# A diffusion block's feed-forward: gate folded into the second weights, sums begun as the residual, context products kept in two PSUM banks

## The chip, the cores and the metric

One core of a Trainium2 chip runs the whole kernel. The metric is the device time of one execution in microseconds (us). Five engines work side by side, each with its own queue that it works off in order: PE (matrix products), ACT, DVE and POOL (element by element), and SP, which here issues loads. POOL issues the stores and some loads.

## The reference, cut to what matters

One layer runs over 128 context tokens and 2,048 latent tokens, 17 tiles of 128. The change lies in the feed-forward part and the end:

```python
h = rmsnorm(x, norm2_g) * (1 + scale2) + shift2
x = x + gate2 * (jnp.square(jax.nn.relu(h @ w_ff1)) @ w_ff2)
...
y_prompt = rmsnorm(y_p, final_g)
y_sample = rmsnorm(y_s, final_g)
```

`w_ff1` is 1024 x 4096 and `w_ff2` 4096 x 1024. `gate2` has 1,024 columns, one row for the context token tile and one for all latent tiles. Ahead of it lie the mixing part and its output projection (`out_proj`).

## The kernel before, in words

Every product of two f32 operands is made of three matmuls (`mm3`, L179): both operands are split into a high and a low part (`split`, `operand`), and high x high, high x low and low x high are added in one PSUM bank. Over this the latent tiles use a seven-product scheme for 2 x 2 blocks: sums of operand blocks are formed first, seven products (numbered p = 0 to 6) are made, and their results are added up.

**FF1** (L1330 to L1391) makes `relu(h @ w_ff1)**2`. Its outer loop g runs over two halves of the latent tokens, its inner loop i over 16 slices of 256 columns of `w_ff1`; one pair (g, i) is called a step here. A step (`ff1_units`, L1249) has 7 products of 4 units, 84 matmuls of 512 columns in all, and in the first half (g = 0) also 24 matmuls of 256 columns for the context tile. Products 0, 2, 4 and 6 add up in one bank (`za`), 3 and 5 in another (`zc`): product 4 can't start before the sum after product 2 has been copied out. These sums go to three buffers, `fx` (two of it), `fy` and `fz` (one each): f00 and f10 in `fx`, f01 and f11 in `fz`; POOL forms the operand sums of FF2 in `fy` and `fz` (`comb`, L1265), and POOL's queue stores all three to DRAM (`f_d`, L1287, L1292, L1293). While a step runs, the weights of the next are loaded, added and split (`left_operand`), and twice in the second half `w2_prep` (L1347) forms sums of `w_ff2`'s blocks for FF2 on POOL and stores them in `w2_d`.

**FF2** (L1396 to L1599) runs over 8 chunks c of 512 rows of `w_ff2`, and in each over four blocks b of four token tiles with 28 units, 84 matmuls, each, and a fifth, the context tile (`ff2_context`, 24 matmuls). `operand` loads each operand (SP), casts it on ACT (L1413) and subtracts on DVE or POOL by turns (L1414). `put` (L1447) adds each finished bank to the tile's sum `ya` on DVE, or in the first and last chunk copies it on ACT (L1459). `whole` (L1465) runs in the last two chunks: it multiplies the sum by the gate row (DVE), adds the residual `x1_d` or the older sum (POOL), and in the last chunk squares (ACT) for the final norm. `norm` (L1485) scales and stores.

The order of the work is written out by hand in `weave` (L154): a list of PE's units, and beside it items with the unit number ahead of which each is put in the program. The framework may still move an instruction that isn't pinned with `keep_in_program_order`; matmuls and the `ld_in_order` loads are pinned. A tile of a ring waits until all uses of the tile that had its place before are over.

Of the kernel before, what the change touches and what calls it, by code (L numbers as in the profile page):

```python
# [12 lines left out]
ALU = mybir.AluOpType  # L13
# [30 lines left out]
def tile_hybrid(  # L44
# [39 lines left out]
    w2_d = [dram.tile([P, 2, 2, D], F32, name=f"w2_d{c}") for c in range(DFF // 512)]  # L84
# [1096 lines left out]
    for t in range(NT - 2, -1, -1):  # L1181
# [67 lines left out]
    def ff1_units(g, i, w, tb):  # L1249
# [8 lines left out]
        f00, f10, f01, f11 = fx[:, 0], fx[:, 1], fz[:, 0], fz[:, 2]  # L1258
# [9 lines left out]
        def after(p):  # L1268
# [66 lines left out]
    for i, kk in ORDER[4:6]:  # L1335
        right_operand(0, i, kk, TB[0])
# [10 lines left out]
    def w2_prep(i, unit):  # L1347


        box = []  # L1350

        def load():
            for f in range(2):
                box.append(unit())
                ld.dma_start(out=box[f], in_=w_ff2[0, (2 * i + f) * P:(2 * i + f + 1) * P, :])

        def step():
            (x, y), (z, w) = ((b[:, 0:512], b[:, 512:]) for b in box)
            G.tensor_tensor(out=w, in0=w, in1=y, op=ALU.subtract)
            G.tensor_tensor(out=y, in0=y, in1=x, op=ALU.subtract)  # L1360
            G.tensor_tensor(out=x, in0=w, in1=x, op=ALU.add)
            G.tensor_tensor(out=z, in0=z, in1=x, op=ALU.subtract)
            for f in range(2):
                st.dma_start(out=w2_d[i // 2][:, i % 2, f], in_=box[f])

        return load, step

    for g in range(2):
        for i in range(NP):
# [26 lines left out]
    gp = ctx.enter_context(tc.tile_pool(name="gp", bufs=1, reuse_waits="tile"))  # L1396
    CP = 2
    NC_ = NP // CP
    ya, yl, norms, ctr = {}, {}, [], [0]

    def ounit(dt=F32R):
        return gp.tile([P, D], dt, tag="o", name="o", bufs=24)

    def sunit(dt=F32R):
# [225 lines left out]
```

## Time and profile before

| | us |
|---|---|
| median of 3 runs (2595.0 to 2604.34) | 2604.31 |
| the profiled execution | 2596.67 |
| its span, first to last instruction | 2594.9 |
| PE busy | 2319.6 (89%) |
| DVE busy | 1804.1 (70%) |
| POOL busy | 1141.9 (44%) |
| ACT busy | 979.7 (38%) |

The rows below are from this one execution. FF1 runs from about 985 to 1826 us of the span, its second half from about 1402, and FF2 from there to the end. L131 is the line of every matmul, so PE's rows are told apart by their tiles: `z` and `g` are PSUM banks, `T`, `u`, `v`, `o` and `s` operand tiles. A busy PE isn't PE at its peak, since the ends of matmuls are modelled; the number of matmuls in a stretch, in brackets, is the better measure.

### The profile page before, as it was taken

The numbers are of one execution on the slowest core, as the hardware profiler recorded it, in microseconds if no ns is written. First come the engines' busy times: TensorE is split into PE (matmuls) and PEld (weight loads), VectorE is DVE, ScalarE is ACT, GpSimd is POOL, SyncE is SP. The second block draws the span as 40 slices with busy tenths as digits, with TensorE's granted clock in tenths as the row PEclk, the third lists the DMA queues.
The fourth block names the chain that finished last, engine by engine and source line by source line (L and its number), as shares of the span: only waits on it lengthen the run. The fifth ranks groups of instructions, "written<-read, shape, count | busy, mean of one in ns | idle before, by whom it ended". The sixth has DMA issues, their size and how long they took to land.

```text
span 2594.9 us, 32716 instructions
## 1 busy us (share of the span) xinstructions
PE 2319.6 (89%) x12018; PEld 1876.3 (72%) x12018; DVE 1804.1 (70%) x2632; ACT 979.7 (38%) x1824; POOL 1141.9 (44%) x1023
## 2 busy tenths in 40 slices
PE   7999999999979897999996788888799999999766
PEld 5788887777757675777775566667588778787655
DVE  5987755878878847667766665655347776778887
ACT  4666663333435455322323222222342222222243
POOL 1332225444324454334435633434544554347764
PEclk9999999999989997999998898889899999999888
DMA  8666444333355555343335423333655555455633
GB/s 279 218 216 204 172 153 143 120 122 126 135 189 181 178 196 176 116 140 132 110 132 196 165 100 124 103 121 110 219 177 176 198 207 178 164 182 195 226 124 116
DMA packets 212655, 422.75 MB, mean 163 GB/s; under 512 B 16165, under 2 KB 116815, under 8 KB 208912
## 3 DMA queue, kind: packets, MB, share of 16 engines
q1 hardware_dynamic: 166704, 246.27, 29.0%
q0 software_dynamic: 45792, 174.40, 19.1%
q8 instruction: 95, 1.56, 0.2%
q14 instruction: 64, 0.52, 0.1%
HBM read 267.76 MB, written 152.85 MB: 162 GB/s over the span
## 4 chain that ended last, share of the span: by engine, by line
PE 39%; POOL 16%; DVE 12%; DMA 11%; issue 8%; ACT 4%; POOLq 0%; SPq 0%; DVEq 0%; ACTq 0%
PE z L131 29%; PE g L131 9%; DMA f_d<-fz 6%; POOL fy L1266 4%; POOL fz L1266 4%; DVE cacc L67 3%; DMA o<-f_d 1%; PE g L134 1%; DMA raw<-in_w_ff_dram 1%; POOL o L1414 1%; DVE v L177 1%; DVE fz L67 1%; DMA T<-tb_d 1%; POOL f_d L1287 1%; POOL T L1482 1%
## 5 line engine op out<-in xcount | busy, mean ns | idle before, releaser
L131 PE MATMUL z<-w,hb 128*128 128x512 f32 (+1 forms) x2486 | 564.5, 373 | 13.8 <-ACT hb L776 7.4
L131 PEld LDWEIGHTS z<-w,hb 128*128 128x128 f32 x2486 | 420.0, 191 | 95.5 <-ACT hb L776 7.6
L131 PE MATMUL z<-u,v 128*128 128x512 f32 x1152 | 305.7, 428 | 87.7 <-ACT fz L1275 83.5
L131 PEld LDWEIGHTS z<-u,v 128*128 128x128 f32 x1152 | 238.9, 210 | 154.1 <-ACT fz L1275 96.0
L131 PE MATMUL z<-o 128*128 128x512 f32 x1152 | 299.9, 411 | 54.6 <-ACT o L1459 25.4
L131 PE MATMUL z<-T,v 128*128 128x512 f32 x1152 | 290.2, 405 | 35.9 <-DVE T L1171 13.0
L131 PEld LDWEIGHTS z<-o 128*128 128x128 f32 x1152 | 227.5, 199 | 111.2 <-ACT o L1459 27.5
L131 PEld LDWEIGHTS z<-T,v 128*128 128x128 f32 x1152 | 221.6, 194 | 90.2 <-DVE T L1171 13.8
L131 PE MATMUL g<-o 128*128 128x512 f32 x1152 | 278.9, 391 | 0.8 <-DVE T L1461 0.7
L1413 ACT CAST o<-o 128x1024 fp32r<-128x1024 f32 x128 | 134.3, 1051 | 384.6 <-DMA o<-f_d 276.4
L131 PEld LDWEIGHTS g<-o 128*128 128x128 f32 x1152 | 217.5, 189 | 48.5 <-DVE T L1461 1.3
L1266 POOL TENSOR_TENSOR fy<-fz 128x512 f32<-128x512 f32 x32 | 60.2, 1880 | 424.8 <-DVE fz L67 424.8
L67 DVE SCALAR_TENSOR_TENSOR cacc<-xp,wd,cacc 128x512 f32<-128x512 f32 (+2 forms) x360 | 237.4, 713 | 0.0
L1414 POOL TENSOR_TENSOR o<-o 128x1024 fp32r<-128x1024 f32 x49 | 120.2, 2452 | 204.7 <-ACT o L1413 204.4
L1461 DVE TENSOR_TENSOR T<-T,z 128x512 f32<-128x512 f32 x212 | 141.9, 681 | 72.9 <-PE z L131 72.7
L131 PE MATMUL z<-w,T 128*128 128x512 f32 x720 | 183.5, 409 | 7.4 <-POOL T L777 3.8
L1461 DVE TENSOR_TENSOR T<-T,g 128x512 f32<-128x512 f32 x167 | 113.5, 683 | 80.2 <-PE g L131 68.4
L1414 DVE TENSOR_TENSOR o<-o 128x1024 fp32r<-128x1024 f32 x79 | 139.5, 1766 | 36.8 <-ACT o L1413 36.8
L131 PEld LDWEIGHTS z<-w,T 128*128 128x128 f32 x720 | 136.1, 194 | 38.6 <-POOL T L777 4.7
L177 DVE TENSOR_TENSOR v<-cacc,v 128x1024 fp32r<-128x1024 f32 x64 | 98.6, 1542 | 73.1 <-PE z L131 73.1
L177 DVE TENSOR_TENSOR v<-raw,v 128x1024 fp32r<-128x1024 f32 x64 | 117.2, 1832 | 42.6 <-PE z L131 40.0
L131 PE MATMUL z<-o,s 128*128 128x512 f32 x528 | 132.1, 402 | 13.5 <-DVE T L1461 6.8
(317 smaller groups left out, 3795.6 us busy)
## 6 DMA issues: line engine op xcount, KB each, us to landing
raw<-in_w_ff_dram SPq DMA_DIRECT2D x116, 512.0 KB
o<-f_d SPq DMA_DIRECT2D x96, 512.0 KB
f_d<-fz POOLq DMA_DIRECT2D x32, 768.0 KB, 5.9
raw<-in_w_mod_dram SPq DMA_DIRECT2D x32, 512.0 KB
f_d<-fy POOLq DMA_DIRECT2D x32, 512.0 KB, 3.5
f_d<-fx POOLq DMA_DIRECT2D x32, 512.0 KB, 3.6
o<-w_d SPq DMA_DIRECT2D x32, 512.0 KB
hb<-hT_d POOLq DMA_DIRECT2D x15, 1024.0 KB, 5.7
```

What stands on the lines that cost most here:

```text
L67: return V.scalar_tensor_tensor(out=out, in0=in0, scalar=scalar, in1=in1, op0=op0, op1=op1)
L131: tc.keep_in_program_order(T.matmul(out, lhsT, rhs, start=start, stop=stop, skip_group_check=read))
L134: tc.keep_in_program_order(T.transpose(out, in_, ident if idn is None else idn))
L177: order(V.tensor_tensor(out=lo, in0=src, in1=hi.bitcast(F32), op=ALU.subtract))
L1266: G.tensor_tensor(out=out, in0=a, in1=b, op=op)
L1287: st.dma_start(out=dst[:, 2:4], in_=fy)
L1413: S.copy(out=hi, in_=lv)
L1414: (G if ctr[0] % 2 else V).tensor_tensor(out=lo, in0=lv, in1=hi.bitcast(F32), op=ALU.subtract)
L1461: V.tensor_tensor(out=o_, in0=o_, in1=bank, op=ALU.add)
L1482: eng.tensor_tensor(out=y[:, fs], in0=y[:, fs], in1=tmp, op=ALU.add)
```

## The change: what it does, and the diff

In FF1, f01 is kept in `fy` and the copy of product 3 too; only the sum after product 4 goes to `fz`. The three POOL sums stand in another order. The right operand i = 2 of the first half is loaded while `out_proj` works on tile 0, and the first operands of FF2 in the last step of FF1. `w2_prep` multiplies the rows of `w_ff2` by the latent gate row on POOL and stores all seven combinations of each, so `w2_operand` reads them all from `w2_d`. In FF2 every sum `ya` begins as the residual, loaded from `x1_d` in the first chunk, and each bank is added on DVE; `put` and `whole` are gone. The context tile's fifth block is gone: in each block b two units (six matmuls) on plain rows of `w_ff2` add to two PSUM banks that are held through all of FF2, and its gate and residual are applied at the end. Cut to what matters:

```diff
-    w2_d = [dram.tile([P, 2, 2, D], F32, name=f"w2_d{c}") for c in range(DFF // 512)]
+    w2_d = [dram.tile([P, 2, 7, 512], F32, name=f"w2_d{c}") for c in range(DFF // 512)]
...
-        if t in (3, 1):
+        if t in (3, 1, 0):
 
-            items += [(10 + 4 * kk, lambda kk=kk, i=(3 - t) // 2: right_operand(0, i, kk, TB[0])) for kk in range(2)]
+            items += [((10 if t else 5) + 4 * kk, lambda kk=kk, i={3: 0, 1: 1, 0: 2}[t]: right_operand(0, i, kk, TB[0]))
+                      for kk in range(2)]
...
-        f00, f10, f01, f11 = fx[:, 0], fx[:, 1], fz[:, 0], fz[:, 2]
+        f00, f10, f01, f11 = fx[:, 0], fx[:, 1], fy[:, 1], fz[:, 2]
...
             elif p == 3:
-                S.copy(out=f11, in_=zc)
+                S.copy(out=fy[:, 0], in_=zc)
             elif p == 4:
-                V.tensor_tensor(out=f11, in0=f11, in1=za, op=ALU.add)
+                V.tensor_tensor(out=f11, in0=fy[:, 0], in1=za, op=ALU.add)
                 square(f11)
             elif p == 5:
                 V.tensor_tensor(out=f01, in0=f01, in1=zc, op=ALU.add)
                 square(f01)
+                comb(fz[:, 0], f00, f01, ALU.subtract)
                 comb(fy[:, 1], f01, f11, ALU.add)
                 comb(fy[:, 0], fy[:, 1], f00, ALU.subtract)
-                comb(fz[:, 0], f00, f01, ALU.subtract)
                 st.dma_start(out=dst[:, 2:4], in_=fy)
...
-    for i, kk in ORDER[4:6]:
-        right_operand(0, i, kk, TB[0])
...
-    def w2_prep(i, unit):
+    def w2_prep(i, unit, g2):
...
-                ld.dma_start(out=box[f], in_=w_ff2[0, (2 * i + f) * P:(2 * i + f + 1) * P, :])
+                ld_in_order(out=box[f], in_=w_ff2[0, (2 * i + f) * P:(2 * i + f + 1) * P, :])
+
+        def gate():
+            for x in box:
+                G.tensor_tensor(out=x, in0=x, in1=g2, op=ALU.mult)
+            st.dma_start(out=d_[:, 0], in_=box[0][:, 0:512])
+            for f, p in ((0, 1), (1, 5)):
+                st.dma_start(out=d_[:, p], in_=box[1][:, f * 512:f * 512 + 512])
...
+            for p, o in ((2, x), (4, y), (3, w), (6, z)):
+                st.dma_start(out=d_[:, p], in_=o)
...
+            if (g, i) == (1, NP - 1):
+
+                items += [(x, lambda n=n: f_operand(0, 0, n, F, tunit)) for x, n in ((5, 0), (9, 1), (15, 2))]
+                items.append((11, lambda: w2_operand(0, 0, w2, tunit)))
+            if g == 1 and i == 3:
+                g2f = raw()
+                gate_row(g2f, 1, 1)
             if g == 1 and i in (4, 8):
-                items += zip((3, 12), w2_prep(i // 4 - 1, lambda: tunit(F32)))
+                items += zip((3, 10, 22), w2_prep(i // 4 - 1, lambda: tunit(F32), g2f))
...
-            put(c, t, hs, bank, first)
-            if p == 1:
-                whole(c, e, 0)
...
+            y = ya[t][:, (left, right)[h]]
+            V.tensor_tensor(out=y, in0=y, in1=bank, op=ALU.add)
+            if last and p in (1, 4, 5, 6):
+                square(t, h)
+            if last and norms and (p < 5 or b == 3):
                 norm(norms.pop(0))
...
+    def residual(b):
+
+        for t in sum([[e, e - 1] for e in tiles_of(b)], []):
+            ya[t] = tunit(F32)
+            ld_in_order(out=ya[t], in_=x1_d[t])
...
-    def ff2_context(c, F, w2):
...
+    yc = [zbank(), zbank()]
+
+    def context(c, b, Fc):
...
+        def load():
+            rw = raw()
+            k = 2 * CP * c + b
+            ld_in_order(out=rw, in_=w_ff2[0, k * P:(k + 1) * P, :])
+            box.extend([ounit(), ounit()])
+            split_two(*box, rw)
+
+        def unit(h):
+            hs = (left, right)[h]
+            mm3(yc[h], *Fc[b % 2, b // 2], box[0][:, hs], box[1][:, hs], c + b == 0, (c, b) == (NC_ - 1, 3), True)
...
+    w2_operand(0, 1, w2)
+    residual(0)
+    for p in range(2, 7):
         w2_operand(0, p, w2)
+    f_operand(0, 0, 3, F)
+    fc_operand(0, Fc)
...
-        for b in range(5):
+        for b in range(4):
             items, Fn = [], {}
-            units = ff2_units(c, b, F, w2) if b < 4 else ff2_context(c, F, w2)
+            units = ff2_units(c, b, F, w2)
+            cload, cunits = context(c, b, Fc)
+            units[16:16] = cunits
+            items.append((3, cload))
...
+            if b == 0 and c > 0:
+                items += wl(c, (0.5, 5), (5, 6), w2)
+            if c == 0 and b < 3:
+                items.append((8, lambda: residual(b + 1)))
+            if b in (0, 1) and more:
+                items += zip((6, 12, 26), w2_prep(CP * (c + 1) + b, raw, g2r))
```

`split_two` casts on ACT and subtracts on POOL or DVE by turns, as `operand` did. The gate row is held in one of the three `raw` tiles (`g2f`) in FF1 and in a `cacc` tile in FF2.

## Rows read from the trace of the kernel before

**Rows 1.** Busy time by stage (start:end, span; engines; granted clock, DMA share, GB/s).

```profile
1052.90:1360.00 307.10, 290.44 (x1401) 240.16 (x1400) 211.57 (x203) 89.34 (x128) 121.58 (x103) 0.99 0.39 128
1445.00:1826.00 381.00, 318.81 (x1256) 254.93 (x1255) 225.13 (x217) 86.69 (x114) 144.50 (x112) 0.90 0.34 120
1827.00:1872.00 45.00, 28.84 (x86) 20.91 (x87) 16.83 (x13) 15.64 (x21) 28.03 (x18) 0.77 0.65 220
1934.00:2352.70 418.70, 411.89 (x1806) 337.82 (x1805) 297.79 (x356) 114.60 (x122) 198.60 (x121) 1.00 0.56 187
2352.70:2595.00 242.30, 184.13 (x718) 145.66 (x716) 201.00 (x245) 77.07 (x141) 164.61 (x113) 0.87 0.48 163
```

**Rows 2.** Waits of PE: total us, times, longest.

```profile
PE z L131 <- ACT fz L1275: 83.5, 29, 6.2
PE z L131 <- ACT o L1459: 28.5, 6, 7.2
```

**Rows 3.** Timeline, two steps of FF1's second half (start, us, engine, what, idle before).

```profile
1615.08 0.59 ACT L1275 COPY fz<-z 128x512 f32<-128x512 f32 x1 [10.01 <-DMA f_d<-fz]
...
1615.72 9.91 PE L131 MATMUL z<-u,v 128*128 128x512 f32 x36 [3.98 <-ACT fz L1275]
...
1625.47 2.93 PE L131 MATMUL z<-T,v 128*128 128x512 f32 x12
...
1625.91 2.21 POOL L1266 TENSOR_TENSOR fy<-fz 128x512 f32<-128x512 f32 x1 [15.61 <-DVE fz L67]
...
1631.47 0.75 POOL L1287 DMA_DIRECT2D f_d<-fy  x1
...
1634.43 0.77 POOL L1293 DMA_DIRECT2D f_d<-fz  x1
1636.51 1.23 DVE L177 TENSOR_TENSOR v<-cacc,v 128x1024 fp32r<-128x1024 f32 x1 [2.20 <-PE z L131]
...
1640.42 0.59 ACT L1275 COPY fz<-z 128x512 f32<-128x512 f32 x1 [10.45 <-DMA f_d<-fz]
```

**Rows 4.** Timeline, PE in two steps of FF1's first half.

```profile
1184.55 8.45 PE L131 MATMUL z<-u,v 128*128 128x512 f32 x36 [1.12 <-ACT fz L1275]
...
1208.23 8.46 PE L131 MATMUL z<-u,v 128*128 128x512 f32 x36 [1.11 <-ACT fz L1275]
```

**Rows 5.** Timeline, PE in FF1's first step.

```profile
999.48 0.80 PE L131 MATMUL z<-T,v 128*128 128x512 f32 x1 [4.18 <-ACT T L1170]
```

**Rows 6.** Page, DMA issues: KB each, us to landing.

```profile
f_d<-fy POOLq DMA_DIRECT2D x32, 512.0 KB, 3.5
```

**Rows 7.** Timeline, end of FF1 and start of FF2.

```profile
1826.52 0.37 SPq L137 DMA_DIRECT2D o<-f_d  x1
...
1833.52 2.35 POOL L1414 TENSOR_TENSOR o<-o 128x1024 fp32r<-128x1024 f32 x1
1835.83 2.36 POOL L1414 TENSOR_TENSOR o<-raw,o 128x1024 fp32r<-128x1024 f32 x1
...
1835.93 4.63 PE L131 MATMUL z<-o 128*128 128x512 f32 x10 [4.16 <-POOL o L1414]
```

**Rows 8.** Groups of POOL instructions from 1840 to 2350 us (busy, mean ns).

```profile
L1414 POOL TENSOR_TENSOR o<-o 128x1024 fp32r<-128x1024 f32 x38 | 92.0, 2421 | 195.3 <-ACT o L1413 195.1
...
L1362 POOL TENSOR_TENSOR raw<-raw 128x512 f32<-128x512 f32 x12 | 23.3, 1943 | 0.9
...
L1364 POOL DMA_DIRECT2D w_d<-raw x24 | 13.4, 558 | 0.0
```

**Rows 9.** Groups of DVE instructions from 1840 to 2350 us.

```profile
L1461 DVE TENSOR_TENSOR T<-T,z 128x512 f32<-128x512 f32 x177 | 118.6, 682 | 59.9 <-PE z L131 59.7
```

**Rows 10.** Line 1414 from 1840 to 2350 us (ns min/median/max).

```profile
L1414 DVE TENSOR_TENSOR o<-o x62: 1211/1226/4055, 1842.8 to 2349.7; 128x1024 fp32r<-128x1024 f32 x62
```

**Rows 11.** Groups of ACT instructions from 2470 to 2595 us.

```profile
L64 ACT ACTIVATE o<-T 128x512 f32<-128x512 f32 x34 | 21.5, 632 | 50.1 <-POOL T L1482 47.9 <-DVE T L1482 2.3
```

**Rows 12.** Groups of DVE instructions from 2470 to 2595 us.

```profile
L67 DVE SCALAR_TENSOR_TENSOR T<-T,ssq,cacc 128x512 f32<-128x512 f32 x34 | 31.0, 945 | 11.3 <-POOL ssq L166 11.3
```

**Rows 13.** Timeline, PE's last products.

```profile
2577.82 4.60 PE L131 MATMUL z<-o,s 128*128 128x512 f32 x12 [3.11 <-ACT o L1459]
```

More of the change, by code (lines that the diff above doesn't have):

```diff
@@ new lines, in w2_prep, with ounit, sunit, split_two @@
+        return load, gate, step
+    CP = 2
+    NC_ = NP // CP
+    gp, ya, yl, norms, ctr = [], {}, {}, [], [0]
+    w2, F, Fc = {}, {}, {}
+    def ounit(dt=F32R):
+        return gp[0].tile([P, D], dt, tag="o", name="o", bufs=24)
+    def sunit(dt=F32R):
+        return gp[0].tile([P, 512], dt, tag="s", name="s", bufs=6)
+    def split_two(hi, lo, src):
+        ctr[0] += 1
+        S.copy(out=hi, in_=src)
+        (G if ctr[0] % 2 else V).tensor_tensor(out=lo, in0=src, in1=hi.bitcast(F32), op=ALU.subtract)
@@ L1363, in step, with fc_operand @@
+    def fc_operand(c, out):
+        x = operand(fc_d[c].rearrange("p q f n -> p (q f) n"), sunit)
+        for q in range(2):
             for f in range(2):
-                st.dma_start(out=w2_d[i // 2][:, i % 2, f], in_=box[f])
-        return load, step
+                out[f, q] = [y[:, (2 * q + f) * P:(2 * q + f + 1) * P] for y in x]
     for g in range(2):
@@ L1391, in tile_hybrid @@
     fps.close()
[L1396 to L1404, printed above, removed]
-        return gp.tile([P, 512], dt, tag="s", name="s", bufs=6)
-    def operand(src, unit, via=None):
-        hi, lo = unit(), unit()
-        lv = lo.bitcast(F32) if via is None else via()
-        ld_in_order(out=lv.rearrange("p (a n) -> p a n", a=src.shape[1]), in_=src)
-        ctr[0] += 1
-        S.copy(out=hi, in_=lv)
-        (G if ctr[0] % 2 else V).tensor_tensor(out=lo, in0=lv, in1=hi.bitcast(F32), op=ALU.subtract)
-        return hi, lo
@@ L1427, in f_operand @@
[L1427 to L1440 removed]
+    gp.append(ctx.enter_context(tc.tile_pool(name="gp", bufs=1, reuse_waits="tile")))
@@ L1442, in tile_hybrid @@
     fgr = cacc()
     ld.dma_start(out=fgr, in_=final_g.unsqueeze(0).broadcast_to([P, D]))
-    g2rows = {1: cacc()}
-    gate_row(g2rows[1], 1, 1)
-    def put(c, t, hs, bank, first):
-        last = c == NC_ - 1
-        if last:
-            if t not in yl:
-                yl[t] = ounit(F32)
-            o_ = yl[t][:, hs]
-        else:
-            if t not in ya:
-                ya[t] = tunit(F32)
-            o_ = ya[t][:, hs]
-        if first and (last or c == 0):
-            S.copy(out=o_, in_=bank)
-        else:
-            V.tensor_tensor(out=o_, in0=o_, in1=bank, op=ALU.add)
@@ L1463, in tile_hybrid @@
[L1463 to L1483 removed]
+    g2r = cacc()
@@ new lines, in tile_hybrid, with tiles_of, square @@
+    gate_row(g2r, 1, 1)
+    left, right = slice(0, 512), slice(512, 1024)
+    def tiles_of(b):
+        return [NT - 1 - 8 * (b // 2) - 4 * (b % 2) - 2 * j for j in range(2)]
+    def residual(b):
+        for t in sum([[e, e - 1] for e in tiles_of(b)], []):
+            ya[t] = tunit(F32)
+            ld_in_order(out=ya[t], in_=x1_d[t])
+    def square(t, h):
+        if t not in yl:
+            yl[t] = const.tile([P, 2], F32, name="ssq4", bufs=8)
+        fs = (left, right)[h]
+        act(raw4[0][:, fs], ya[t][:, fs], AF.Square, accum_out=yl[t][:, h:h + 1])
@@ L1497, in ff2_units @@
     def ff2_units(c, b, F, w2):
-        units = []
         banks = {}
-        tt = [NT - 1 - 8 * (b // 2) - 4 * (b % 2) - 2 * j for j in range(2)]
+        tt = tiles_of(b)
+        last = c == NC_ - 1
         def after(p, j):
```

162 lines of the change are left out of this document (57 added, 105 removed).

## The prediction

> **What bounds the kernel now.** I read the busy time by stage first, then PE's waits, then the timeline inside the stages that lose time. By stage [rows 1] PE runs 1,806 matmuls in 411.89 busy us in FF2's chunks 1 to 5, so 0.228 us for one of 512 columns at granted clock 1.00, the 2.4 GHz level. A stage is judged against that price. Chunks 1 to 5 take 418.7 / 5 = 83.7 us each, against 360 x 0.228 = 82.1: PE bounds them. FF1's second half takes 381 / 15 = 25.4 us a step (1,256 matmuls recorded, 15 x 84 = 1,260) against 84 x 0.228 = 19.15. The first block of FF2 takes 45 us for 84 matmuls, and the last two chunks and the tail 242.3 us for 720, that is for 164.2. In these three the granted clock is 0.90, 0.77 and 0.87, so some of the time ran at 1.2 GHz.
>
> PE's waits [rows 2] name two causes: 83.5 us in 29 waits for the copy of line 1275 (f01 into `fz`), and 28.5 us in 6 for the copies of line 1459, which `put` makes in the last chunk. The timeline of FF1 [rows 3] shows the first. The copy sits on ACT until the store of the previous step's `fz` has landed: issued at 1634.43, copy at 1640.42. Product 4 needs the same bank, so PE stands. A step is then a loop: landing, products 4 to 6, POOL's sums, store, landing; 25.3 us from one copy to the next. In the first half the context tile's 24 matmuls lie inside the loop, and the wait is 1.1 us [rows 4] at clock 0.99.
>
> **FF1's second half.** After the change f01 is copied to `fy`, whose store comes earlier. Counted from product 0 at 1625.47 [rows 3], POOL starts at +0.4, issues the `fy` store at +6.0 and the `fz` store at +9.0. The new order of the three sums has the same three sums ahead of the first. The `fy` store takes 3.5 us to land [rows 6], so the place is free at +9.5 and the copy done at +10.1. Product 4 is due at 4 x 12 x 0.228 = +10.9, so this wait would be gone, with 0.8 us to spare. `fz` is needed only for the sum after product 4, at +13.7; its store lands at +15.0 (the copy at 1640.42 shows it), and product 6, which needs the bank, is due at +16.4: the sum of 0.7 us [rows 9] just fits. Next late is the low part of a weight: DVE writes it at 1636.51 to 1637.74, +11.0 to +12.3, after a wait of 2.2 us for PE. Product 4's third matmul would want it at +11.4, if this is the weight of product 4 and keeps its place: 0.9 us. With 0.4 us for DVE, which is blocked in front of `fz`'s sum from +13.7 to +15, a step is 19.15 + 1.3 = 20.5. The term is 15 x (25.4 - 20.5) = -74. Bounds: 19.2 a step (-93), or half of the difference kept, 22.3 (-47).
>
> The two `w2_prep` of this half grow. Each gets 2 POOL products of 1,024 columns; no row shows a POOL product with a gate row, so I bound it by the split of the same width, 2.42 us, and by twice the 512-column difference, 3.9 [rows 8], and take 2.4, since it is the same shape. Its stores go from 2 to 7 at 0.56. That is 4.8 + 2.8 = 7.6 us each on POOL, which works 144.50 / 15 = 9.6 us in a step [rows 1] and so has about 11 free. If a gate stands ahead of the sums, PE pays. The gate row also holds one of the three `raw` tiles, so a load of weights starts up to half a step later, ahead of ACT's casts. +8 for both (0 if POOL's gap covers it, +25 if each costs most of a step).
>
> **FF1's first half and start.** The first half has the same loop and loses its 1.1 us in 14 steps: -15 (0 to -16). At the start PE waits 4.2 us for a cast of the right operand that is now made earlier [rows 5]: -5 (0 to -10). The two loads and splits move behind the output projection's POOL work and delay nothing that I see; if POOL is late there, the gain is 0.
>
> **FF2's first block.** PE is through with FF1 at about 1826.5, when the next operand load is let go [rows 7], and then waits mostly for operands. Now product 0's operands are split before that, so PE goes on. Product 1's low part is on POOL, behind FF1's last sums and stores, which let POOL go at 1833.52: ready at 1835.9, 9.4 us after FF1. From there PE needs 72 x 0.228 = 16.4, and the rest of the operands come at the pace of casts of 1 us, so the block ends 26 to 27 us after FF1, not 45: -18 (-8 if the loads behind the four residuals on SP come late, -24 if nothing is missed).
>
> **Chunks 0 to 5.** Matmuls stay the same: 24 of the context in each chunk either way. POOL's work grows from 198.6 / 5 = 39.7 us a chunk [rows 1] by two context splits (4.8), four gate products (9.6) and 10 stores (5.6): about 60 of 82, so it doesn't bound by sum. DVE gets two more splits and loses three sums and some more, about even at 297.8 / 5 = 59.6. SP's loads gain the context's plain rows and lose nothing; DMA was at a share of 0.56. Three orders can cost. A context split given to POOL stands behind the second part of `w2_prep`, 4 differences and 4 stores, about 8 us, and is wanted after 16 of 30 units, 10.9 us. The next `raw` loads wait for those stores, and the FF2 operands behind them on SP. And the two context banks are held, so only two `z` banks are left for product 0: at each block's start it waits for the sum of product 6, 0.69 us [rows 9], with 6 matmuls, 1.37 us, as cover; a DVE split in front of it (1.23 us at the median [rows 10]) uncovers about half a us. Against this go 1.6 us of today's loss a chunk. I take +10 over six chunks (-8 to +35).
>
> **Chunks 6 and 7 and the tail.** `whole` goes: 64 gate products on DVE and 64 adds on POOL, and the copies on ACT that wait behind squares, which themselves waited 47.9 us for POOL's adds [rows 11]. Chunk 6 becomes like chunk 5, 83.7. Chunk 7 has no `w2_prep`, but DVE makes 14 sums of 0.69, about 4 us of splits and four norms a block. A norm is two products of 0.945 us and a wait of 11.3 / 17 [rows 12], 2.6 us, and all four are called in the first four units after a block: 10.4 us of DVE beside 5.5 us of PE. PE has cover of some 6 us before product 4 wants a bank, so about 2.5 us are lost in each of three blocks: 82 + 8 = 90. The tail was 2594.9 - 2582.4 = 12.5 us after the last product [rows 13] and becomes about 11: a sum, a square, two norms, a store. Together 185 against 242.3: -57 (-42 to -66).
>
> **The sum.** -5 - 15 - 74 + 8 - 18 + 10 - 57 = -151, from the profiled execution's 2596.67 to 2446. That execution is 7.6 us below the median of the runs shown, 2604.31, and close to the lowest, 2595.0; I give 2445 and leave the offset to the range. About 0.5%, 13 us, is what a measurement of this kernel can tell from no change.
>
> **A rule against it.** DVE's split of 1,024 columns takes 1.23 us at the median and 1.21 at the least, but 4.06 at the most [rows 10]: now and then it is held up by about a POOL split (2.42 us), mostly it isn't. The Trainium skill (SBUF — State Buffer, section Who interferes with whom) says that a DVE instruction with two SBUF inputs and a GpSimd one that reads SBUF exclude each other for the whole instruction. By that rule, POOL's 20 us more a chunk would meet a quarter of the 14 DVE splits and hold each up by half an instruction, 4 us of DVE a chunk; if all of it reached PE, six chunks would cost 24 us more and the sum would be 2470. The long instances agree with it; the median shows that it is rare here.
>
> **The rivals.** First, **a new wait in FF1's loop**: `fy`'s landing or the late weight takes over. For it: margins of 0.8 and 0.7 us, and DVE at 225 of 381 us and blocked in order. Against it: the `fy` store is issued 3 us before the `fz` store and lands 2.4 us faster. With half of the gain gone, 36 + 8 more: about 2490; chance 0.18. Second, **POOL's queue in FF2's chunks**: the context split and the loads behind `w2_prep` stop PE by about 8 us in each of seven chunks, 56 less the 10 counted: 2491; chance 0.18. Third, **all covers hold**: second half 19.2 a step, `w2_prep` free, chunks 82.1, first block at its best: 2446 - 19 - 8 - 20 - 6 = 2393; chance 0.14. Fourth, **slower than before by the held banks**: at each of 31 block borders both halves of product 0 wait behind a DVE split at its longest, 4.06 + 0.69 - 1.37 = 3.4 us each, 6.8 a border, 210 us and so 2656. It decides from 151 / 31 = 4.9 us a border. Against it: the median split is a third of that, and a split ready early is placed after the sums. Chance 0.03. That the wait of line 1275 goes on as it was, because the framework keeps ACT behind `fz` all the same, would leave 2446 + 89 = 2535; nothing in the code does this: 0.02.
>
> **How the numbers follow.** The forecast has 0.45, from 2415 to 2475 by its own terms. The range takes in half of the third case and the first two: 2390 to 2515; about 0.18 is left out, above and below. Faster by over 0.5% are all cases but the fourth and some mixture of the second with a poor start: 0.95; same 0.02, slower 0.03.
>
> **What would show it.** Right: the wait of PE for line 1275 below 10 us in all; 84 matmuls each 20 to 21 us in FF1's second half, clock 0.97 or more; first FF2 block below 30 us; no line 1459; POOL about 60 us in a chunk of 83 to 86; last two chunks and tail 180 to 195. Wrong: a step above 22 us with PE waiting for DVE's weights or the copy into `fy`; PE waiting for POOL's context split at unit 16 of block 1; PE waiting for DVE at block borders for over 2 us.

## The result, and the profile after

The changed kernel takes 2481.26 us in the median of four runs (2473.83 to 2484.8), the kernel before 2604.32 beside it: a ratio of 0.9532, interval 0.9501 to 0.9562. Direction and range held; the gain is 123 us instead of the 159 forecast. The profiled execution's span goes from 2594.9 to 2480.1 us, 114.8 less. The stages are cut at POOL's stores of `fz`, which end a step of FF1, and at PE's products in FF2:

| stretch | before | after | difference | predicted |
|---|---|---|---|---|
| to the first `fz` store | 1034.1 | 1038.2 | +4.1 | -5 |
| FF1, first half, 15 steps | 388.3 | 367.0 | -21.3 | -15 |
| the step between the halves | 32.6 | 26.5 | -6.1 | 0 |
| FF1, second half, 15 steps | 377.7 | 311.7 | -66.0 | -66 |
| FF2, first block | 45.0 | 42.3 | -2.7 | -18 |
| FF2, the rest of chunks 0 to 5 | 480.7 | 503.8 | +23.1 | +10 |
| FF2, chunks 6 and 7, tail | 242.3 | 196.9 | -45.4 | -57 |

(FF2's first row begins where FF1's last matmul ends; half a us lies between the landmarks.) FF1 gave 89 us, FF2 25 where 65 were forecast.

The busy time by stage of the changed kernel (columns as in [rows 1]): FF1's halves, the first block of FF2, chunks 1 to 5, and the rest.

```profile
1066.20:1405.20 339.00, 322.23 (x1558) 269.30 (x1556) 260.35 (x236) 112.60 (x154) 152.71 (x129) 0.97 0.45 148
1431.70:1743.40 311.70, 291.39 (x1239) 235.91 (x1237) 229.38 (x212) 93.76 (x120) 162.47 (x134) 0.97 0.51 174
1737.10:1779.40 42.30, 26.07 (x92) 19.96 (x91) 19.66 (x19) 14.81 (x16) 38.17 (x29) 0.80 0.98 357
1844.80:2288.90 444.10, 421.00 (x1811) 341.35 (x1810) 336.62 (x352) 134.84 (x140) 314.86 (x202) 0.99 0.65 217
2288.90:2480.10 191.20, 164.52 (x700) 132.34 (x698) 137.65 (x207) 64.72 (x112) 93.82 (x66) 0.95 0.54 186
```

In chunks 1 to 5 POOL now works 315 of 444 us, 63 a chunk (it was 39.7), as forecast; the chunk takes 88.8 us instead of 83.2 (from one cast of a `raw` operand in the chunk's first block to the same one of the next chunk, mean of five; the figure used for chunks from here on). In the first block DMA is at a share of 0.98.

The waits of PE:

```profile
PE z L131 <- DVE T L1498: 24.3, 20, 3.2
PE z L131 <- DVE o L1389: 21.2, 7, 8.3
PE z L131 <- ACT fy L1276: 15.0, 5, 6.6
...
PE g L131 <- POOL o L1389: 6.4, 1, 6.4
```

Both lines of [rows 2] are gone: 112 us of waits. In their place stand DVE's sums into the residual (L1498), the low parts of operands (L1389) and some of the copies into `fy`. The timeline of a quiet step of FF1's second half answers to [rows 3]:

```profile
1639.15 2.88 PE L131 MATMUL z<-T,v 128*128 128x512 f32 x12
...
1645.47 0.75 POOL L1288 DMA_DIRECT2D f_d<-fy  x1 [0.30 <-POOL fy L1267]
...
1649.53 0.59 ACT L1276 COPY fy<-z 128x512 f32<-128x512 f32 x1 [5.92 <-DMA f_d<-fy]
...
1650.17 8.45 PE L131 MATMUL z<-u,v 128*128 128x512 f32 x36
...
1658.46 2.88 PE L131 MATMUL z<-T,v 128*128 128x512 f32 x12
```

ACT still waits for a landing, now that of `fy`, 4.1 us after its issue; the copy ends at +10.97 from product 0, and product 4 starts at +11.02 without a wait. The step takes 19.31 us, the price of its 84 matmuls.

FF2's first block waits for operands (timeline, first block and, last two rows, what was late):

```profile
1746.65 5.06 PE L131 MATMUL g<-o,T 128*128 128x512 f32 x11 [6.44 <-POOL o L1389]
...
1767.67 2.50 PE L131 MATMUL z<-o,s 128*128 128x512 f32 x5 [8.29 <-DVE o L1389]
...
1744.23 7.00 POOL L1389 TENSOR_TENSOR o<-o 128x1024 fp32r<-128x1024 f32 x3
...
1765.33 2.29 DVE L1389 TENSOR_TENSOR o<-raw,o 128x1024 fp32r<-128x1024 f32 x1
```

Product 1's low part stands behind FF1's last sums on POOL, as forecast, but the context's split ends at 1767.6, so PE stands again after one matmul of the context. And in the first block of chunk 3 (chunks are counted from 0):

```profile
2030.06 3.55 DVE L1389 TENSOR_TENSOR o<-o 128x1024 fp32r<-128x1024 f32 x1
...
2034.13 4.55 DVE L1389 TENSOR_TENSOR o<-o 128x1024 fp32r<-128x1024 f32 x1
...
2030.11 2.41 POOL L1359 TENSOR_TENSOR raw<-raw,cacc 128x1024 f32<-128x1024 f32 x1
...
2033.96 2.42 POOL L1389 TENSOR_TENSOR o<-o 128x1024 fp32r<-128x1024 f32 x1
...
2036.33 1.27 POOL L1366 TENSOR_TENSOR raw<-raw 128x512 f32<-128x512 f32 x1
...
2038.74 4.38 PE L131 MATMUL z<-o,s 128*128 128x512 f32 x11 [2.30 <-DVE o L1389]
```

A split that DVE does in 1.22 us alone takes 3.55 beside a gate product of POOL's, and 4.55 beside a split and a difference that follow each other on POOL. PE stands 2.3 us for the second, and its next 11 matmuls take 4.38 us instead of 2.65 (12 take 2.88 elsewhere): over those 6.6 us the granted clock is 0.74, and 1.00 before and after.

### The profile page after: what moved, and what is told of

It reads as the page before. It is cut to its first block, busy times and chain, and to the rows that moved or that the text cites. A ratio compares the mean times of both kernels' runs of the same rounds, so it can differ in the third digit from the quotient of the medians.

```text
span 2480.1 us, 33032 instructions
## 1 busy us (share of the span) xinstructions
PE 2270.2 (92%) x12018; PEld 1852.5 (75%) x12018; DVE 1818.1 (73%) x2624; ACT 980.4 (40%) x1788; POOL 1216.4 (49%) x1087
## 5 line engine op out<-in xcount | busy, mean ns | idle before, releaser
L1388 ACT CAST o<-o 128x1024 fp32r<-128x1024 f32 x148 | 155.6, 1051 | 433.1 <-DMA o<-f_d 297.3
L131 PE MATMUL z<-u,v 128*128 128x512 f32 x1152 | 282.8, 404 | 31.9 <-ACT fy L1276 15.0
L131 PE MATMUL z<-o 128*128 128x512 f32 x1080 | 265.4, 393 | 20.9 <-DVE T L1498 20.8
L131 PEld LDWEIGHTS z<-o 128*128 128x128 f32 x1080 | 201.2, 188 | 72.1 <-DVE T L1498 28.2
L1267 POOL TENSOR_TENSOR fz<-fx,fy 128x512 f32<-128x512 f32 x64 | 99.4, 1554 | 294.2 <-DVE fy L67 293.1
L1498 DVE TENSOR_TENSOR T<-T,z 128x512 f32<-128x512 f32 x256 | 171.7, 682 | 96.4 <-PE z L131 95.8
L1389 POOL TENSOR_TENSOR o<-o 128x1024 fp32r<-128x1024 f32 x71 | 177.1, 2503 | 120.3 <-ACT o L1388 119.9
L1389 DVE TENSOR_TENSOR o<-o 128x1024 fp32r<-128x1024 f32 x77 | 159.9, 2078 | 26.0 <-ACT o L1388 17.8
L1498 DVE TENSOR_TENSOR T<-T,g 128x512 f32<-128x512 f32 x192 | 129.3, 683 | 67.3 <-PE g L131 66.8
L131 PE MATMUL z<-o,s 128*128 128x512 f32 x576 | 150.3, 405 | 23.2 <-DVE o L1389 19.7
L177 DVE TENSOR_TENSOR v<-raw,v 128x1024 fp32r<-128x1024 f32 x64 | 131.1, 2050 | 29.5 <-PE z L131 28.1
L131 PEld LDWEIGHTS z<-o,s 128*128 128x128 f32 x576 | 112.1, 196 | 50.6 <-DVE o L1389 22.2
```

The lines of the kernel that those rows point to most:

```text
L131: tc.keep_in_program_order(T.matmul(out, lhsT, rhs, start=start, stop=stop, skip_group_check=read))
L177: order(V.tensor_tensor(out=lo, in0=src, in1=hi.bitcast(F32), op=ALU.subtract))
L1267: G.tensor_tensor(out=out, in0=a, in1=b, op=op)
L1388: S.copy(out=hi, in_=src)
L1389: (G if ctr[0] % 2 else V).tensor_tensor(out=lo, in0=src, in1=hi.bitcast(F32), op=ALU.subtract)
L1498: V.tensor_tensor(out=y, in0=y, in1=bank, op=ALU.add)
```

## The experiments

Two theories stood at first. **P**: in FF2, POOL's added work (gate products first) holds up DVE's splits, so operands and sums come late. **Z**: the two `z` banks held for the context make PE wait for DVE at block borders.

**FF1's part alone, on the kernel before.**

```diff
-        f00, f10, f01, f11 = fx[:, 0], fx[:, 1], fz[:, 0], fz[:, 2]
+        f00, f10, f01, f11 = fx[:, 0], fx[:, 1], fy[:, 1], fz[:, 2]
...
-                S.copy(out=f11, in_=zc)
+                S.copy(out=fy[:, 0], in_=zc)
...
-                V.tensor_tensor(out=f11, in0=f11, in1=za, op=ALU.add)
+                V.tensor_tensor(out=f11, in0=fy[:, 0], in1=za, op=ALU.add)
...
+                comb(fz[:, 0], f00, f01, ALU.subtract)
                 comb(fy[:, 1], f01, f11, ALU.add)
                 comb(fy[:, 0], fy[:, 1], f00, ALU.subtract)
-                comb(fz[:, 0], f00, f01, ALU.subtract)
```

> The kernel before with one part of the change alone: FF1's partial sums f01 and zc's copy placed in fy, f11 in fz, and the store order that goes with it. Nothing of FF2 is touched and the second weights are not gated. Theory (the placement alone makes FF1's gain, 85 to 90 us of the 123): 2604 falls to 2510 to 2520, the step of FF1's second half goes from 25.5 to 19.5 to 20.5 us, the first half's from 23.7 to 22.2, and since the preparations here have no gate products, the two disturbed pairs cost under 12 us in all instead of 21. Rival (a good part of FF1's gain came from operands that were prepared earlier, or from the stores' order of the other parts): a gain under 60 us, steps of the second half above 22 us.

2486.0 us, ratio 0.956 (0.9537 to 0.9583): not to be told from the whole change (0.9501 to 0.9562). The stages of this run, the second half of FF1 and a stretch of FF2 of five chunks' length, from the third block of chunk 0 on:

```profile
1433.90:1723.20 289.30, 284.16 (x1235) 230.66 (x1233) 220.17 (x212) 89.23 (x115) 139.05 (x112) 1.00 0.45 156
...
1782.80:2195.80 413.00, 407.45 (x1788) 334.59 (x1787) 280.07 (x335) 122.61 (x139) 199.32 (x120) 1.00 0.56 189
```

The gain is more than expected, since the second half falls to 289.3 us: the placement is worth 377.7 - 289.3 = 88 us there, and the heavier preparations of the second weights in the changed kernel take back 22. FF2 (last `fz` store to last product) is 748 us here, as before, and 722 in the changed kernel. So the rest of the change nets 4 us by the spans (2484.1 and 2480.1): 26 less in FF2, 2 more in the tail, 20 more in FF1.

**No gate products.**

```diff
-            for x in box:
-                G.tensor_tensor(out=x, in0=x, in1=g2, op=ALU.mult)
```

> The changed kernel without the two gate products of w2_prep (four of seven products of the second weights are so not gated; all loads, differences and stores stay, and so do all bytes). Theory (POOL's gate products, 2.4 to 2.9 us each, run beside DVE's splits, which then take 2.2 to 4.5 us instead of 1.2, so that product 6's operand and the puts come late): chunks 1 to 5 fall from 88.4 to 83 to 85 us, the 2.2 us wait in each first block goes, the first block of FF2 from 42 to 37 to 39, and FF1's second half loses 8 to 12 of its 21 us of disturbance: 2481 falls to 2435 to 2450. Rival Z (the two z banks held by the context sums make PE wait for DVE at block borders): chunks stay at 87 to 88.5, only FF1's part comes, 2470. Rival D (bytes: more and larger transfers in each chunk): as the bytes stay, nothing changes in FF2, 2470 to 2481.

2474.69 us, 0.9517 (0.9486 to 0.9549): the figures of the rivals Z and D. FF1's second half falls to 300.0. FF2 stays, 723.5, and so does the chunk, 88.9: the theory's first form failed. In the middle chunks (1800 to 2280 us) the waits for operands go and those for sums grow, to 25.1 us in 14, most of them at block borders; the changed kernel has 12.5 in 12 for sums and 11.4 in 5 for operands. The timeline at one of them says why:

```profile
2045.14 4.63 DVE L1387 TENSOR_TENSOR s<-s 128x512 fp32r<-128x512 f32 x1
2049.70 1.27 DVE L1496 TENSOR_TENSOR T<-T,g 128x512 f32<-128x512 f32 x2
...
2044.50 4.72 POOL L1387 TENSOR_TENSOR o<-o 128x1024 fp32r<-128x1024 f32 x2
...
2051.62 4.50 PE L131 MATMUL z<-o 128*128 128x512 f32 x12 [3.94 <-DVE T L1496]
```

A split of 512 columns takes 4.63 us beside two splits of POOL's in a row and ends 0.55 us after them. So it isn't the gate products alone that hurt: two splits of POOL's do the same, and the sum queued behind the split on DVE frees the bank that PE waits for. A sum, one operand in PSUM, takes 0.67 to 0.69 us in FF2's chunks in every run. The Trainium skill (SBUF — State Buffer, section Who interferes with whom) has DVE and GpSimd (POOL here) exclude each other when DVE has two SBUF inputs and GpSimd reads SBUF: this row agrees, and so do the sums.

In FF1 the edit moved something else too. The loads of a preparation are issued 7.1 us ahead of a store of `fz`, in the changed kernel 1.5 us, and that store lands 5.8 to 6.1 us after its issue instead of 9.1 to 9.2. So the 12 us that FF1 gains here aren't all the gate products'.

**The turns of DVE and POOL swapped.**

```diff
+    ctr[0] += 1
     w2_operand(0, 1, w2)
```

> The changed kernel with the turn of DVE and POOL in the splits of FF2 swapped (one count added before the first operand made after FF1), so that product 6's low part is POOL's and the others change hands too. Theory (POOL's added work is what comes late): product 6's split now stands behind the gate products in POOL's own queue, so the wait of PE in each first block moves from DVE o to POOL o and is no shorter than 2 us; the time is 2475 to 2500. Rival Z (held banks): the same waits for DVE's puts at the borders, 2478 to 2484. A gain of over 10 us would say that the choice of engine for single operands is what costs, not the sum of the work.

2543.8 us, 0.9787 (0.975 to 0.9823), slower than any theory gave. Chunks take 99.9 us. The context's split is DVE's now and ends 1.1 us after a gate product of POOL's:

```profile
1949.62 2.77 DVE L1389 TENSOR_TENSOR o<-raw,o 128x1024 fp32r<-128x1024 f32 x1
...
1947.88 3.42 POOL L1359 TENSOR_TENSOR raw<-raw,cacc 128x1024 f32<-128x1024 f32 x1
...
1952.44 2.50 PE L131 MATMUL z<-o,s 128*128 128x512 f32 x5 [3.62 <-DVE o L1389]
```

With the same work, which operand falls to which engine moves 62 us. Only the first block gains, 31.5 us instead of 42.3.

**The preparations in the second and third block.**

```diff
-            if b in (0, 1) and more:
-                items += zip((6, 12, 26), w2_prep(CP * (c + 1) + b, raw, g2r))
+            if b in (1, 2) and more:
+                items += zip((0, 6, 13), w2_prep(CP * (c + 1) + b - 1, raw, g2r))
```

> The changed kernel with the preparations of the second weights in the second and third block of each chunk (units 0, 6 and 13) instead of the first and second (units 6, 12 and 26): the same work, away from the block that waits for product 6. Theory (gate products beside DVE's splits of that block): the wait of 2.2 us and the half clock behind it go from the first blocks, FF2's first block loses its 8.3 us wait for the context's split or most of it, chunks 85 to 87 us, 2481 falls to 2450 to 2470. Rival Z (held banks): no change, 2478 to 2484. If the waits come back in the second or third block with the same size, the amount of POOL's work beside DVE's counts and not its place.

2480.09 us, 0.9539 (0.9506 to 0.9571), the chunk 89.1. From 1800 to 2280 us PE waits once for an operand (1.0 us), and 28.1 us in 19 for sums, most of them at block borders: 29 us in all, where the changed kernel has 24. As the last sentence on record has it, between these two places the amount counts.

**All splits on DVE.**

```diff
-        (G if ctr[0] % 2 else V).tensor_tensor(out=lo, in0=src, in1=hi.bitcast(F32), op=ALU.subtract)
+        V.tensor_tensor(out=lo, in0=src, in1=hi.bitcast(F32), op=ALU.subtract)
```

> The changed kernel with every split of FF2 on DVE (in the changed kernel they go to DVE and POOL in turn); POOL keeps the preparation of the second weights alone. Theory P (a DVE split, two operands in SBUF, stands still as long as POOL works beside it: 4.6 us for a 128x512 split beside two of POOL's, and the puts queued behind it come late): with POOL at 20 us in a chunk instead of 53 the splits take 1.2 to 1.5 us on the mean instead of 2.2, DVE is at 28 x 1.2 + 56 x 0.68 = 72 of 84 us, the waits for DVE in chunks 1 to 5 shrink and FF2 goes from 722 to 690 to 712: 2450 to 2470. Rival B (DVE's sum of work is the bound): at 72 of 84 us and with 14 more splits in its queue the puts come later than now, FF2 730 to 770, 2490 to 2530.

2520.79 us, 0.9698 (0.9682 to 0.9715), the chunk 95.8: rival B's figures. The next run takes POOL away altogether.

**The same without preparations in FF2.**

```diff
-        x = operand(w2_d[c][:, :, p], unit)
+        x = operand(w2_d[0][:, :, p], unit)
...
-            if b in (0, 1) and more:
-                items += zip((6, 12, 26), w2_prep(CP * (c + 1) + b, raw, g2r))
```

> The run with all of FF2's splits on DVE, and besides without the preparations of the second weights in FF2, so that POOL does nothing there (chunks 1 to 7 read the first chunk's products: all second weights after the first chunk are left out of the output; the bytes that the preparations moved are left out too, the operands' loads stay). With the preparations the chunk took 97 us, a split of 128x1024 on DVE 1.44 us on the mean and of 128x512 1.42 us, and PE stood 6.2 to 7.8 us in each first block for the context's split. Theory P (a split on DVE stands still while POOL works): all splits of 128x1024 take 1.21 to 1.25 us, those of 128x512 0.65 to 0.75, the wait in the first block falls to under 2 us, chunks 82 to 86 us, 2420 to 2445. Rival B (DVE's work and the order of its queue): splits may be shorter, but the wait in each first block stays over 4 us and chunks over 90 us, 2470 to 2500.

2464.49 us, 0.9485 (0.9455 to 0.9516), the chunk 88.4, between the two forecasts. The instructions of the split's line from 1845 to 2289 us (ns min/median/max): with POOL idle, with POOL's preparations (the run above), and in the changed kernel, where POOL has half of the splits besides.

```profile
L1389 DVE TENSOR_TENSOR o<-o x96: 1216/1220/1228, 1845.1 to 2287.9; 128x1024 fp32r<-128x1024 f32 x96
L1389 DVE TENSOR_TENSOR s<-s x25: 683/685/687, 1853.0 to 2276.2; 128x512 fp32r<-128x512 f32 x25
```

```profile
L1389 DVE TENSOR_TENSOR o<-o x86: 1211/1221/3418, 1848.7 to 2284.1; 128x1024 fp32r<-128x1024 f32 x86
L1389 DVE TENSOR_TENSOR s<-s x23: 679/687/2892, 1844.7 to 2270.0; 128x512 fp32r<-128x512 f32 x23
```

```profile
L1389 DVE TENSOR_TENSOR o<-o x50: 1211/1516/5761, 1853.7 to 2283.4; 128x1024 fp32r<-128x1024 f32 x50
L1389 DVE TENSOR_TENSOR s<-s x16: 687/1698/2912, 1845.6 to 2287.5; 128x512 fp32r<-128x512 f32 x16
```

With POOL idle the longest split is 1% over the shortest, so the long ones are POOL's doing: P's mechanism holds. But PE still stands 2.8 us in each first block for the context's split, so P doesn't make up the 88 us of that kernel. What does isn't shown apart: 28 splits and 56 sums on one queue, B's part, and the two banks, which this run holds too. The run also has less DMA traffic (a share of 0.46 instead of 0.59), which it can't tell from POOL's idleness in the time; in the splits' durations it can, since in all three runs a split of 1,024 columns exceeds 1.25 us only where a product, split or difference of POOL's runs beside it.

**No bank held.**

```diff
-    yc = [zbank(), zbank()]
...
-            mm3(yc[h], *Fc[b % 2, b // 2], box[0][:, hs], box[1][:, hs], c + b == 0, (c, b) == (NC_ - 1, 3), True)
+            mm3(gbank(), *Fc[b % 2, b // 2], box[0][:, hs], box[1][:, hs], True, True)
...
-                V.tensor_tensor(out=tmp[:, hs], in0=yc[h], in1=tmp[:, hs], op=ALU.mult)
+                V.tensor_tensor(out=tmp[:, hs], in0=tmp[:, hs], in1=tmp[:, hs], op=ALU.mult)
```

> The changed kernel whose context products go to a g bank that nobody reads, so that no z bank is held (the context row's second layer is left out of the output; PE, loads and splits do the same work). Rival Z (two of four z banks are held, so a block can't begin before the last put of the block before): the waits of PE for DVE's puts, 24 us in 20 places, fall under 5 us and with them the half clock behind them, FF2 goes from 722 to 685 to 705, 2445 to 2465. Theory P alone (late operands, DVE beside POOL): the waits for DVE's splits stay at 21 us, the puts' waits fall a little, FF2 710 to 722, 2470 to 2481. If both waits go, the banks are what turns a late split into a stall.

2459.89 us, 0.9455 (0.943 to 0.948), FF2 706.9, the chunk 86.0. Of FF2's waits for sums 19.2 us in 13 are left, not under 5. In the middle chunks they stay (12.8 us in 7, where the changed kernel has 12.5 in 12), but the waits for operands, 11.4 us in 5, are gone. So what was on record, that both waits go, holds in the first block of each middle chunk alone: there the changed kernel waits once for a sum and once for a split, and this one not at all; its waits stand in later blocks. FF2's first block stays at 42.3.

**One `z` and one `g` bank held.**

```diff
-    yc = [zbank(), zbank()]
+    yc = [zbank(), gbank()]
```

> The changed kernel with the context sums held in one z bank and one g bank instead of two z banks; the same work, the whole output. With no z bank held FF2 fell from 722 to 707 us and the waits for DVE's puts in the middle chunks stayed at one per chunk. Theory Z (a third z bank gives the next block its first bank before the last put of the block before): FF2 705 to 714, 2462 to 2474, and the border waits left are those where a split of DVE stands beside a run of POOL's. Rival (the g banks are as short: four are asked for in each block, now of three): FF2 720 to 735, with waits of PE for DVE on g, 2480 to 2495.

2463.18 us, 0.9479 (0.9462 to 0.9497), FF2 707.2, the chunk 86.0: the whole of the gain with the whole of the output. From 1800 to 2280 us PE waits 15.6 us in 6 places, one in the second block of each chunk. The start of chunk 3 shows what the bank does. First the changed kernel, then this run:

```profile
2016.28 2.67 DVE L1389 TENSOR_TENSOR o<-o 128x1024 fp32r<-128x1024 f32 x1
...
2019.60 1.65 PE L131 MATMUL z<-o 128*128 128x512 f32 x6 [1.25 <-DVE T L1498]
```

```profile
2010.17 2.68 DVE L1389 TENSOR_TENSOR o<-o 128x1024 fp32r<-128x1024 f32 x1
...
2010.73 2.88 PE L131 MATMUL z<-o 128*128 128x512 f32 x12
```

The split is stretched as far in both. In the changed kernel the sum behind it comes 1.25 us too late for PE's second half of product 0; with a third `z` bank PE goes on. Bytes, rival D of the run without gate products, can't be this gain: they are the same here (DMA share 0.66, 0.65 in the changed kernel). The mean of DVE's splits of 1,024 columns falls as well, from 2.37 us to 1.69, but a shorter split alone does little: without the gate products it is 1.80 us on the mean, with two `z` banks held, and the chunk stays at 88.9.

**FF1's preparations spread, and retimed.** First spread over two steps:

```diff
             if g == 1 and i in (4, 8):
-                items += zip((3, 10, 22), w2_prep(i // 4 - 1, lambda: tunit(F32), g2f))
+                pl, pg, ps = w2_prep(i // 4 - 1, lambda: tunit(F32), g2f)
+                items += [(3, pl), (10, pg)]
+            if g == 1 and i in (5, 9):
+                items.append((6, ps))
```

> The changed kernel with each of the two preparations of the second weights in FF1 spread over two steps: load and gate products as before, the four differences and their stores at unit 6 of the next step instead of unit 22 of the same. Theory (in a step of 19.3 us POOL has 10 us free; gate products and differences together take 15 to 18 and push the combinations and fy's store back, so ACT's next copy into fy waits): the disturbed pairs cost 4 to 6 us in all instead of 22, FF1's second half 293 to 297 instead of 312, 2481 falls to 2462 to 2468. Rival (the seven stores and their bytes disturb it, not POOL's queue): 305 to 312, 2474 to 2481.

2481.95 us, 0.9546 (0.9531 to 0.956), the second half 314.3: nothing gained, as the edit did not take effect. The differences (L1366 to L1369) run straight behind the gate products all the same, and the next step's sums behind them:

```profile
1479.34 2.35 POOL L1359 TENSOR_TENSOR T<-T,raw 128x1024 f32<-128x1024 f32 x1
1481.99 1.13 POOL L1362 DMA_DIRECT2D w_d<-T  x2 [0.30 <-POOL T L1359]
1483.14 1.41 POOL L1366 TENSOR_TENSOR T<-T 128x512 f32<-128x512 f32 x1
...
1490.89 1.30 POOL L1267 TENSOR_TENSOR fz<-fx,fy 128x512 f32<-128x512 f32 x1
```

An item's place in the source is not its place in POOL's queue. So the second edit pins them:

```diff
+                items.append((11, pl))
+            if g == 1 and i in (5, 9):
+                items.append((3, pg))
+            if g == 1 and i in (6, 10):
+                items.append((3, ps))
...
-                G.tensor_tensor(out=x, in0=x, in1=g2, op=ALU.mult)
+                tc.keep_in_program_order(G.tensor_tensor(out=x, in0=x, in1=g2, op=ALU.mult))
...
-            G.tensor_tensor(out=y, in0=w, in1=y, op=ALU.subtract)
+            tc.keep_in_program_order(G.tensor_tensor(out=y, in0=w, in1=y, op=ALU.subtract))
```

> The changed kernel with the two preparations in FF1 retimed: the loads at unit 11 of the step (they were at unit 3, just when the stores of the step before, fy, fx and fz, are in flight), the gate products at unit 3 of the next step and the differences at unit 3 of the one after, each held behind the instruction traced before it on POOL (in the run that only spread them over two steps, the differences ran straight behind the gate products all the same, 1483 to 1489 us, and the combinations behind both). Theory (the loads lie beside fz's store, which lands 8 us after its issue instead of 6, and POOL's run of 14 us pushes the combinations back): FF1's second half 293 to 302 instead of 312 to 314, 2464 to 2473. Rival (POOL's products cost where they stand, by holding DVE's sums and splits): 305 to 315, 2474 to 2485.

2465.13 us, 0.9485 (0.9472 to 0.9498), but the second half only falls to 307.6, the rival's figure: two bad steps of 27 to 29 us, each with one of 22 behind it, become eight of 21 to 24. In the four of them that have gate products or differences on POOL, the cause is the same as in FF2, a split of a weight beside POOL's work:

```profile
1514.09 5.16 DVE L177 TENSOR_TENSOR v<-cacc,v 128x1024 fp32r<-128x1024 f32 x1 [1.57 <-PE z L131]
...
1513.41 4.74 POOL L1359 TENSOR_TENSOR T<-T,raw 128x1024 f32<-128x1024 f32 x2
...
1521.35 2.83 PE L131 MATMUL z<-u,v 128*128 128x512 f32 x11 [1.10 <-DVE fz L1280]
```

These four take 6.9 us more than 19.3 each. The other four take 10.9 us more, and POOL has no preparation there. In this half the edit left the loads where they were: they are issued 1.4 us ahead of the store of `fz` (1.5 in the changed kernel), and the store lands 9.3 and 9.5 us after its issue instead of 5.8. The sum into `fz` waits for it, and PE for the sum:

```profile
1467.59 1.14 SPq L137 DMA_DIRECT2D T<-in_w_ff_dram  x2
...
1469.03 0.77 POOL L1294 DMA_DIRECT2D f_d<-fz  x1
...
1478.48 0.69 DVE L1280 TENSOR_TENSOR fz<-fy,z 128x512 f32<-128x512 f32 x1 [4.98 <-DMA f_d<-fz]
...
1479.22 4.60 PE L131 MATMUL z<-u,v 128*128 128x512 f32 x12 [2.38 <-DVE fz L1280]
```

So the first of the theory's two terms, the late landing, wasn't tested by this run. The pins may also act in FF2, which is 716.6 here, against 722 in the changed kernel and 727 in the run that only spread; as the last two have the same FF2 and differ by 5, this isn't shown.

**The swap in the first chunk alone.**

```diff
+    ctr[0] += 1
     w2_operand(0, 1, w2)
...
             weave(units, items)
+            if c + b == 0:
+                ctr[0] += 1
```

> The changed kernel with the turn of DVE and POOL swapped in the splits of FF2's first chunk alone. In the run with all turns swapped the first block took 31.5 us instead of 42.3 and the third 26.1 instead of 20.5. Theory (the first block is long because product 1's low part stands in POOL's queue behind FF1's last combinations, and the context's split comes late): the first block takes 30 to 33 us, the first chunk 100 to 103 instead of 106, the rest as in the changed kernel, 2473 to 2479. Rival (what the first block gains, the next chunk gives back in waits for operands): 2478 to 2490.

2474.09 us, 0.9511 (0.9481 to 0.9541), FF2 719.4. The first block takes 32.1 us instead of 42.3. Two late splits changed hands: PE waits 1.4 us for product 1's instead of 6.4, and 1.9 for the context's instead of 8.3, so product 1's place in POOL's queue was worth about half of the 10 us. Some 7 are given back in later blocks. By time it can't be told from the changed kernel.

**The last three together** (banks, retimed preparations, swap in the first chunk).

> Three edits together: the context sums in one z and one g bank, FF1's preparations retimed, and the turn of DVE and POOL swapped in the first chunk of FF2. If they add up by the theories: FF1's second half 295 to 302, FF2 702 to 712, 2445 to 2462. If each only moves a wait to the next one: 2465 to 2480.

2443.93 us, 0.9403 (0.9389 to 0.9417): faster than the change and than any single edit. FF1's second half is 308.6, above its forecast, FF2 698.0, below it, the chunk 85.3. PE's waits from 1800 to 2280 us:

```profile
PE z L131 <- POOL o L1389: 5.9, 5, 2.2
PE z L131 <- DVE T L1503: 5.5, 7, 1.1
PE z L131 <- DVE o L1389: 4.2, 1, 4.2
```

## Why the prediction was right, and where it was wrong

**FF1's wait and its size: right.** The wait of 83.5 us was a loop through the store of `fz`, and the placement alone ends it. The step was put at 20.5 us and is 19.3 where nothing disturbs it: the late weight (0.9) and DVE's block in front of `fz`'s sum (0.4) cost nothing. `fy` lands in 4.1 us instead of 3.5, and the margin of 0.8 us shrinks to 0.05: the first rival missed by that.

**The preparations in FF1: mis-sized.** "+8 for both" measured +22 (311.7 against 289.3), near the upper bound of 25. The step that failed is the count by POOL's free time, "and so has about 11 free". POOL's gap is time in which DVE's splits run, and they stand still while POOL works. And the landing isn't in the sum at all: with the preparation's loads just ahead of it, `fz`'s store lands 9.1 to 9.2 us after its issue, twice, instead of 5.8. That -74 + 8 met the measured -66 is luck: -88 and +22 are two errors that cancel.

**FF1's first half and start.** -15 measured -21.3, outside its bounds (0 to -16). A step fell from 23.7 to 22.2 us: the wait of 1.1 us went, and the same matmuls took 0.4 us less (36 of them 8.32 us instead of the 8.45 of [rows 4]); the prediction counted the wait alone. The start was put at -5 and measured +4.1; across the runs the first `fz` store falls at 1033.5 to 1040.6, so the start is within what varies.

**FF2's first block: wrong.** -18 measured -2.7. The first wait came where the prediction put it, product 1 behind FF1's last sums on POOL, 9.5 us after FF1. But "From there PE needs 72 x 0.228 = 16.4" left out the context's unit in the middle of the block: its split ran last of four on DVE, three of them stretched to 2.3 to 2.8 us. The wait at that unit had been given to POOL's queue, as the second rival; it stood in DVE's.

**Chunks 0 to 5: mis-sized, inside the bounds.** +10 measured +23. Of the three orders named, PE's waits show the third, the held banks with a DVE split ahead of the sum. The other two (POOL's second part, the loads) don't show: from 1800 to 2280 us PE waits for DVE alone. The step that failed is "a DVE split in front of it (1.23 us at the median [rows 10]) uncovers about half a us". The median became 1.52 us, the longest 5.76. Under "A rule against it" the prediction had 24 us more, so +34, and set it aside because "the median shows that it is rare here"; the measured +23 lies between the two. That reading was wrong for the kernel before already. In the stretch of [rows 10] its splits of 1,024 columns took 1.72 us on the mean, 19 of 62 over 2 us, and all seven of 512 columns on DVE were long (0.685 us alone):

```profile
L1414 DVE TENSOR_TENSOR o<-o 128x1024 fp32r<-128x1024 f32 x62 | 106.7, 1720 | 35.5 <-ACT o L1413 35.5
...
L1414 DVE TENSOR_TENSOR s<-s 128x512 fp32r<-128x512 f32 x7 | 17.4, 2487 | 1.6 <-ACT s L1413 1.3
```

They cost PE little there, where no bank is held: the chunk took 83.2 us, its matmuls 82.1. In the trace of before POOL worked 199 of 419 us, in that of after 315 of 444, and the mean went to 2.37 us: how often splits collide depends on the very load that the change adds.

**The held banks: the mechanism right, the price low.** The prediction counted half a us at a border. Holding a `g` bank in place of one `z` bank returns 15 us of FF2. The fourth rival's price, 6.8 us at each of 31 borders, is excluded by 24.3 us of waits in 20 places. The two causes act together: POOL makes a split long, and with two banks the sum behind it stops PE. That this is why dropping the gate products or moving them gained nothing in FF2 is argued: no run takes away both POOL's work and the held banks.

**Chunks 6 and 7 and the tail.** -57 measured -45. Line 1459's waits are gone; what `put`'s copies and `whole` were worth apart from each other no run shows. Chunk 6 has the chunks' new price (88.3 instead of 83.7), chunk 7 about 93 instead of 90, and the tail is 14.5 us after the last product instead of 11: four norm products, 2.74 us, stand in DVE's queue ahead of the last sum.

**The range.** By the prediction's own chances 0.12 lies outside it (half of the third case and the last two), not 0.18.

Open: how the 22 us of FF1's preparations divide between DVE's stretched splits and the landing of `fz` beside the preparation's loads (in the spread run issued at 1471.45 and let go of at 1480.79, 9.3 us, against a median of 5.7). In the retimed run, where the two stand in different steps, the steps with the late landing cost 10.9 us and those with POOL's work 6.9. No run moves the loads alone.

## What to carry to other kernels

A store that still reads a buffer belongs in the loop that you draw: moving one partial sum to the buffer that is stored first was worth nearly the whole of this change. POOL's idle time is not free for work if DVE has instructions with two SBUF operands in the same stretch; count POOL's busy time there as time taken from them, and look at the spread of their durations, not at the median. Where two causes feed one wait, undo both before you say that either is harmless.

## What the runs showed of the hardware

In these rows a DVE split stands still not for one POOL instruction but until a run of them that follow each other is over: 5.16 us, ending 1.1 us after two gate products of 4.74 in all, and 4.63 us for half the width beside two POOL splits of 4.72. POOL's instruction needn't have begun first: in the changed kernel a split that begins at 1956.54 us, while POOL issues two stores, takes 4.22 us and ends 1.1 us after the POOL split behind these issues (2.41 us from 1957.26). Beside two such issues alone (2057.42, 1.12 us) a split at 2057.14 takes 1.23 us. With POOL idle, 96 splits lie between 1216 and 1228 ns.

A short stall costs more than itself: after 2.3 us without a matmul, the next 11 took 4.38 us instead of 2.65, with a granted clock of 0.74 over the 6.6 us, so part of them at 1.2 GHz. The wait of 2.3 us is a loss of 4.
